# One encoder block on one core: the dense expert stage loads its weights two tiles at a time

## The chip, the core and the metric

The kernel runs on one core of a Trainium2 chip. The metric is the device time of one execution in microseconds (us), and a smaller one is better. The core's engines, with the profile's short names, are TensorE (PE, with its weight loads as PEld), VectorE (DVE), ScalarE (ACT), GpSimd (POOL) and SyncE (SP). SP does nothing here but issue DMAs, one after the other in a fixed order; POOL and ACT issue some too. All DMAs share 16 DMA engines.

## The reference, cut to what matters

The block normalizes x (512 frames of 2048 values), projects it, runs a recurrent mixer and a sparse attention, adds the result, and ends with an expert layer in which every frame uses 8 heads x 16 experts out of 16,384. The change lies in that last layer:

```python
def blk(args):                       # hx: frames, e: chosen experts, gt: their gates
    hx, e, gt = args
    act = jax.nn.gelu(jnp.einsum('nd,nhkd->nhk', hx, expert_u[e]), approximate=False)
    return jnp.einsum('nhk,nhkd->nd', gt * act, expert_v[e])
```

`expert_u` and `expert_v` are 16,384 x 2048 float32 each, 128 MB each.

## The kernel before

The kernel works in stages, one after the other: projections and mixers (to about 1695 us), routing (which experts each frame uses, to about 2250 us), then the dense stage to the end. The expert layer is split by frames. The first 176 frames (`NG`) are **gathered**: for each slot POOL fetches 128 expert rows of 8192 B, one row to a partition, into a tile `rows` by an indirect DMA (L1038), and DVE reduces them (L1048 for `expert_u`, L1060 for `expert_v`). The other 336 frames (`ND`) are **dense**: they are multiplied with all experts, and a gate matrix `G` with zeros for the experts that were not chosen selects.

The dense stage, `experts` (from L1240), goes through 16 groups of 8 tiles of 128 experts. Of a group, 6 expert tiles are computed here (2 of each 8 were done early, during routing, and their result comes back as `gel<-d_a`): `act` and `pieces` take 16 blocks of 128x128 weights of `pu` against the 336 frames into `mm` (L220 to L222), ACT applies Gelu, DVE multiplies with `G` (L1255), and the product is split into `Wh` and `Wl` (L233, L234). Then 16 output blocks `db` follow, each one weight tile of `pv` against the 8 `Wh`/`Wl` pairs into `wk` (L1290 to L1292), added to `accT` on DVE (L1297).

Both halves take their weights from `load_w`: SP loads a tile `raw` of 128 x 1024 float32, 512 KB, 4096 B to a partition (L201); ACT rounds it to `whi` (L204); DVE makes the rest `wlo` (L205). Each weight tile then feeds 24 matmuls: `whi` times the high part of the frames, `whi` times the low part, `wlo` times the high part, eight times. The high and low parts of the frames in the dense stage are `ph` and `pl`, packed copies of the routing stage's `h2h` and `h2l` (L1007 and L1008, four copies each).

Buffers come from pools. `wd`, opened at the head of `peer`, has 3 `raw`, 2 `whi` and 2 `wlo`; the query projections of routing (`wpq`) use it first, the dense stage goes on with it. When `h2` (which holds `h2h` and `h2l`) has been closed, a pool `wx` with 2 more `raw` and one more pair is opened in its place, so that the dense stage has 5 `raw` and 3 pairs; `load_w` counts tiles to say which pool serves which. The early expert tiles use a third pool `we`.

What sets the order: a scheduler orders each engine's instructions when the program is built, by when it thinks them ready; `high_priority(offset=100)` lets a weight tile's load and split go 100 instructions ahead. On the chip each engine then works strictly in that order and waits on semaphores. The gathered work is fed into the dense stage by `step`, which issues so many slots per weight tile (`rate`), each not before the last `wlo` (`issue_after(self.last)`). The gathers have 3 buffers `rows`.

Of the kernel before, what the change touches and what calls it, by code (L numbers as in the profile page):

```python
# [19 lines left out]
F32 = mybir.dt.float32  # L20
F32R = mybir.dt.float32r
# [3 lines left out]
AF = mybir.ActivationFunctionType  # L25
# [87 lines left out]
def layout(x, norm_mix_g, w_in, shift_mix, w0, w_decay_up, a0, w_icl_up, w_gate_up, k_k, k_a, r_k, ln_x_w, ln_x_b,  # L113
           kv_norm_g, w_uk, w_uv, rel_bias, w_branch_rwkv, w_branch_dsa, w_out, norm_ffn_g, w_peer_query,
           peer_sub_keys, peer_u, peer_v, norm_final_g):
    A = lambda a: np.ascontiguousarray(np.asarray(a))
    x, w_in = np.asarray(x)[0], np.asarray(w_in)[0]
    cols = columns()
    w = w_in[:, np.maximum(cols.reshape(-1), 0)].reshape(D, NTILE, 128)
    w[:, cols < 0] = 0  # L120
    vec = np.zeros((128, NVEC), np.float32)

    def put(n, a):
        o, k = VEC[n]
        vec[:, o:o + k] = np.asarray(a).reshape(k, 128).T
    put("gmix", norm_mix_g)
    sm = np.asarray(shift_mix)[0]
    c27 = cols[:27].copy()
    c27[(c27 >= 3360) | (c27 < 0)] = 0
    put("sm", sm[c27])  # L130
    for n, a in (("a0", a0), ("kk", k_k), ("ka", k_a), ("rk", r_k), ("lnw", ln_x_w), ("lnb", ln_x_b),
                 ("kvg", kv_norm_g), ("gffn", norm_ffn_g)):
        put(n, a)
    bt = np.asarray(rel_bias)[rel_bucket_table()]
    toep = bt[np.arange(512)[None, :] - np.arange(128)[:, None] - 384 + 511]
    kmajor = lambda m: A(m.reshape(-1, 128, m.shape[1] // 128, 128).transpose(2, 1, 0, 3))
    wbr = np.concatenate([np.asarray(w_branch_rwkv)[0], np.asarray(w_branch_dsa)[0]], 0)
    rank = lambda m: A(np.asarray(m)[0].transpose(1, 0, 2).reshape(2, 128, 1024).transpose(1, 0, 2))
    u = np.asarray(peer_u)[0].reshape(128, 128, 16, 128)
    v = np.asarray(peer_v)[0].reshape(128, 16, 8, 16, 128)  # L140
    return {
        "x": A(x), "xT": A(x.T.reshape(16, 128, T).transpose(1, 0, 2)),
        "w_in": A(w.reshape(16, 128, NTILE, 128).transpose(2, 1, 0, 3)),
        "vec": vec, "con": constants(),
        "w0": A(np.asarray(w0).reshape(1, 1024)), "gfin": A(np.asarray(norm_final_g).reshape(1, D)),
        "gffn": A(np.asarray(norm_ffn_g).reshape(1, D)),
        "wdec": A(np.asarray(w_decay_up)[0]), "wicl": A(np.asarray(w_icl_up)[0]), "wgate": A(np.asarray(w_gate_up)[0]),
        "wuk": rank(w_uk), "wuv": rank(w_uv), "toep": A(toep.transpose(2, 0, 1)),
        "wbr": kmajor(wbr),
        "wout": A(np.asarray(w_out)[0].reshape(8, 2, 128, 4, 512).transpose(3, 0, 2, 1, 4)),  # L150
        "wpq": kmajor(np.asarray(w_peer_query)[0]),
        "subk": A(np.asarray(peer_sub_keys)[0].reshape(16, 128, 128).transpose(2, 0, 1)),
        "pu": A(u.transpose(1, 3, 2, 0)),
        "pv": A(v.transpose(1, 3, 0, 2, 4)),
        "ru": A(np.asarray(peer_u)[0]), "rv": A(np.asarray(peer_v)[0]),
    }

# [10 lines left out]
class Kernel:  # L168
    def __init__(self, tc, io, out, dbg=None):
        self.tc, self.nc, self.io, self.out, self.dbg = tc, tc.nc, io, out, dbg or {}  # L170
        self.fins = ExitStack()
        self.wx, self.nw = None, 0
        self.blocks = ((0, 128), (1, 128), (2, ND - 256))

    def pool(self, name, bufs=1, **kw):
# [14 lines left out]
    def load_w(self, src, wp=None):  # L190

        nc = self.nc
        wp = wp or self.wp
        pr = ps = wp
        if self.wx and wp is self.wp:

            pr, ps = wp if self.nw % 5 < 3 else self.wx, wp if self.nw % 3 < 2 else self.wx
            self.nw += 1
        with self.tc.high_priority(offset=100):
            raw = pr.tile([128, 1024], F32, tag="raw", name="raw", bufs=3 if pr is wp else 2)  # L200
            nc.sync.dma_start(raw, src.rearrange("p a b -> p (a b)"))  # L201
            hi = ps.tile([128, 1024], F32R, tag="whi", name="whi")
            lo = ps.tile([128, 1024], F32R, tag="wlo", name="wlo")
            nc.scalar.activation(hi, raw, AF.Copy)  # L204
            self.last = nc.vector.tensor_tensor(lo, raw, hi.bitcast(F32), op=ALU.subtract).ins  # L205
        return hi, lo

    def gemm(self, *a, **k):
# [2 lines left out]
    def pieces(self, ps, w, xs, nk=16, wp=None):  # L211

        nc = self.nc
        for b in range(0, nk, 8):
            hi, lo = self.load_w(w[:, b:b + 8, :], wp)
            for j in range(8):
                k = b + j
                xh, xl = xs(k)
                s = slice(128 * j, 128 * j + 128)
                nc.tensor.matmul(ps, hi[:, s], xh, start=k == 0, stop=False)  # L220
                nc.tensor.matmul(ps, hi[:, s], xl, start=False, stop=False)  # L221
                nc.tensor.matmul(ps, lo[:, s], xh, start=False, stop=k == nk - 1)  # L222
                if j % 4 == 3:
                    yield
# [729 lines left out]
    def peer(self):  # L954
# [2 lines left out]
        v, sc = nc.vector, nc.scalar  # L957
        with ExitStack() as es:
            E = es.enter_context
            self.wp = E(self.pool("wd", 2))  # L960
            gk = self.gk = E(self.pool("gk"))
            self.eid, self.act_, self.gate = [[gk.tile([128, 128 // g[2]], dt, name=f"{n}{i}") for i, g in enumerate(GROUPS)]
                                              for n, dt in (("eid", I32), ("act", F32), ("gate", F32))]
            self.fold = gk.tile([128, 256], F32, name="fold")
# [41 lines left out]
            for a, b in ((0, 2), (2, 6), (6, 11), (11, 16)):  # L1006
                sc.activation(ph[:, a:b], hh[:, a:b, NG:T], AF.Copy)  # L1007
                v.tensor_copy(pl[:, a:b], hl[:, a:b, NG:T])  # L1008
            self.left.close()
            self.hs = lambda k: (ph[:, k], pl[:, k])  # L1010
            self.wx = E(self.pool("wx", 1))
            self.dp = E(self.pool("dense"))
            self.accT = self.dp.tile([128, 16, ND], F32, name="accT")
            self.experts()
# [224 lines left out]
    def experts(self):  # L1239
# [7 lines left out]
        for cg in range(16):  # L1247
            first, last = cg == 0, cg == 15
            G = dp.tile([128, ng, 8, 16], F32, name="G")
            nc.gpsimd.dma_start(G.rearrange("p g e t -> p g (e t)"), self.d_g[:, cg].rearrange("g p f -> p g f"))  # L1250
            W, wait = {}, []

            def gated(j, a):
                a3 = a.rearrange("p (g t) -> p g t", g=ng)
                v.tensor_tensor(a3, a3, G[:, :, j], op=ALU.mult)  # L1255
                wh = dp.tile([128, ND], F32R, name="Wh", bufs=8)
                wl = dp.tile([128, ND], F32R, name="Wl", bufs=8)
                self.split(a, wh, wl)
                W[j] = wh, wl

            js = list(range(8))
            if first:
                js = js[2:6] + js[0:2] + js[6:8]
            for j in js:
                e = 8 * cg + j
                if e in EARLY:
                    a = self.gel.tile([128, ND], F32, tag="gel", name="gel")
                    nc.scalar.dma_start(a, self.d_a[EARLY.index(e)])
                else:
                    a = run(self.act(e, self.mm()))  # L1270
                wait.append((j, a))
                while len(wait) > (2 if first and j in js[:6] else 0):
                    gated(*wait.pop(0))
                if e not in EARLY:
                    self.step(2)
            while wait:
                gated(*wait.pop(0))
            turn = iter(())
            if last:
                for _ in self.items:  # L1280
                    pass
                self.packed.close()
                turn = self.turned()
            for db in range(16):
                ps = self.wk()[:, 0:ND]
                hi, lo = self.load_w(io["pv"][cg, db])
                for j in js:
                    wh, wl = W[j]
                    s = slice(128 * j, 128 * j + 128)
                    mmul(ps, hi[:, s], wh, start=j == js[0], stop=False)  # L1290
                    mmul(ps, hi[:, s], wl, start=False, stop=False)  # L1291
                    mmul(ps, lo[:, s], wh, start=False, stop=j == js[-1])  # L1292
                a = self.accT[:, db]
                if first:
                    sc.activation(a, ps, AF.Copy)
                else:
                    v.tensor_tensor(a, ps, a, op=ALU.add)  # L1297
                next(turn, None)
                self.step()
# [63 lines left out]
```

## Time and profile before

| | before |
|---|---|
| median of 3 runs | 3996.01 us (3995.74 to 4000.47) |
| the profiled execution's own time | 3985.83 us |
| its span (first to last instruction) | 3984.1 us |
| PE busy | 3857.8 us, 97% of the span |
| DVE busy | 2843.3 us, 71% |
| ACT busy | 1398.7 us, 35% |
| DMA | 949.32 MB, mean 238 GB/s |

All numbers of the trace are from the one profiled execution, and its clock starts at the first instruction. A busy share over the whole span says little, since the stages have different limits. The dense stage lasts from 2250.70 us (its first matmul) to the end. `A <- B` in a table of waits reads: A sat idle until B was done.

### The profile page before, as it was taken

What the parts mean: (1) busy time and instruction counts of PE and PEld (TensorE: products, weight loads), DVE (VectorE), ACT (ScalarE), POOL (GpSimd) and SP (SyncE); (2) the same over time, 40 slices, a digit from 0 to 9 for tenths busy, and PEclk for the clock granted to TensorE, in tenths of its full rate; (3) what the DMA queues carried; (4) which work ended last, traced back from release to release, by engine and by line L of the source; (5) the groups of instructions that cost most, each with busy time, mean ns of one, the idle gap of its engine ahead of it and who ended that gap; (6) DMA issues with size and microseconds to landing.
All of it is one profiled execution on the core that took longest, in us unless ns stands there. A gap on an engine that the chain in (4) does not pass through costs nothing.

```text
span 3984.1 us, 57536 instructions
## 1 busy us (share of the span) xinstructions
PE 3857.8 (97%) x22241; PEld 3492.8 (88%) x22241; DVE 2843.3 (71%) x4742; ACT 1398.7 (35%) x2044; POOL 996.7 (25%) x965
## 2 busy tenths in 40 slices
PE   7999999999999999989999999999999999999998
PEld 6877778888887788878899999999999999999997
DVE  5445589444444643289987688989879889899985
ACT  4222323222224522242377533333333333333333
POOL 2000311010103400020166333333333334333320
PEclk9999999999999999999999999999999999999999
DMA  4343952233226443274377799999989999999994
GB/s 151 119 136 117 206 176 88 89 106 103 88 73 208 144 140 144 73 273 152 129 224 248 269 364 378 378 378 383 382 318 397 372 349 387 368 376 374 378 342 153
DMA packets 260275, 949.32 MB, mean 238 GB/s; under 512 B 28240, under 2 KB 79568, under 8 KB 211088
## 3 DMA queue, kind: packets, MB, share of 16 engines
q0 software_dynamic: 81840, 475.10, 32.0%
q1 hardware_dynamic: 130144, 442.62, 31.7%
q10 hardware_dynamic: 48016, 27.92, 2.4%
q8 instruction: 175, 2.87, 0.3%
q14 instruction: 100, 0.82, 0.1%
HBM read 867.56 MB, written 77.89 MB: 237 GB/s over the span
## 4 chain that ended last, share of the span: by engine, by line
PE 57%; issue 17%; DMA 10%; POOL 7%; DVE 7%; ACT 2%; SPq 0%; POOLq 0%; DVEq 0%; ACTq 0%
PE mm L221 10%; PE mm L222 10%; PE mm L220 10%; POOL rows L1038 6%; DMA rows<-in_rv_dram,eid 5%; PE wk L1292 3%; PE wk L1291 3%; PE wk L1290 3%; PE po L220 2%; PE po L221 2%; PE po L222 2%; DVE wlo L205 2%; PE wk L1220 2%; PE wk L876 2%; PE wk L878 1%
## 5 line engine op out<-in xcount | busy, mean ns | idle before, releaser
L204 ACT ACTIVATE whi<-raw 128x1024 fp32r<-128x1024 f32 x758 | 802.8, 1061 | 1820.4 <-PE mm L221 940.3
L205 DVE TENSOR_TENSOR wlo<-raw,whi 128x1024 fp32r<-128x1024 f32 x758 | 927.2, 1224 | 597.5 <-ACT whi L204 525.7
L1292 PE MATMUL wk<-Wh,wlo 128*128 128x336 f32 x2048 | 652.1, 319 | 13.3 <-DVE wlo L205 13.3
L1290 PE MATMUL wk<-Wh,whi 128*128 128x336 f32 x2048 | 651.6, 319 | 10.8 <-ACT Wh L233 10.8
L1291 PE MATMUL wk<-Wl,whi 128*128 128x336 f32 x2048 | 649.3, 317 | 4.2 <-DVE Wl L234 4.2
L222 PE MATMUL mm<-ph,wlo 128*128 128x336 f32 x1536 | 486.5, 317 | 1.8 <-DVE wlo L205 1.7
L220 PE MATMUL mm<-ph,whi 128*128 128x336 f32 x1536 | 484.9, 316 | 1.2 <-ACT ph L1007 1.2
L221 PE MATMUL mm<-pl,whi 128*128 128x336 f32 x1536 | 485.6, 316 | 0.0
L220 PE MATMUL mm<-xh,whi 128*128 128x512 f32 x1168 | 472.9, 405 | 1.6 <-ACT xh L353 1.5
L222 PE MATMUL mm<-xh,wlo 128*128 128x512 f32 x1168 | 468.3, 401 | 6.0 <-DVE wlo L205 6.0
L221 PE MATMUL mm<-xl,whi 128*128 128x512 f32 x1168 | 470.3, 403 | 0.6 <-POOL xl L355 0.5
L1060 DVE SCALAR_TENSOR_TENSOR out<-rows,act,out 128x2048 f32<-128x2048 f32 x173 | 405.7, 2345 | 46.9 <-DMA rows<-in_rv_dram,eid 46.1
L1038 POOL DMA_INDIRECT rows<-in_ru_dram,eid x176 | 272.2, 1547 | 664.7 <-DVE act L1048 484.3
L1048 DVE CUSTOM_DVE_ANT_0 rows<-rows,h2t 128x2048 f32<-128x2048 f32 x176 | 401.3, 2285 | 46.5 <-DMA rows<-in_ru_dram,eid 46.0
L1038 POOL DMA_INDIRECT rows<-in_rv_dram,eid x176 | 286.0, 1625 | 524.4 <-DVE out L1060 444.0
L1292 PEld LDWEIGHTS wk<-Wh,wlo 128*128 128x128 f32 x2048 | 387.1, 189 | 18.3 <-DVE wlo L205 17.1
L1290 PEld LDWEIGHTS wk<-Wh,whi 128*128 128x128 f32 x2048 | 386.2, 189 | 14.9 <-ACT Wh L233 14.2
L1291 PEld LDWEIGHTS wk<-Wl,whi 128*128 128x128 f32 x2048 | 386.9, 189 | 6.5 <-DVE Wl L234 5.6
L222 PEld LDWEIGHTS mm<-ph,wlo 128*128 128x128 f32 x1536 | 288.3, 188 | 2.7 <-DVE wlo L205 2.6
L220 PEld LDWEIGHTS mm<-ph,whi 128*128 128x128 f32 x1536 | 288.7, 188 | 1.8 <-ACT ph L1007 1.8
L221 PEld LDWEIGHTS mm<-pl,whi 128*128 128x128 f32 x1536 | 289.1, 188 | 0.0
L222 PEld LDWEIGHTS mm<-xh,wlo 128*128 128x128 f32 x1168 | 221.7, 190 | 60.2 <-DVE wlo L205 6.9
(441 smaller groups left out, 6348.1 us busy)
## 6 DMA issues: line engine op xcount, KB each, us to landing
raw<-in_pu_dram SPq DMA_DIRECT2D x256, 512.0 KB, 7.7
raw<-in_pv_dram SPq DMA_DIRECT2D x256, 512.0 KB, 8.0
raw<-in_w_in_dram SPq DMA_DIRECT2D x146, 512.0 KB, 3.8
d_g<-Gs ACTq DMA_DIRECT2D x21, 1024.0 KB, 6.8
G<-d_g POOLq DMA_DIRECT2D x16, 1344.0 KB, 15.1
raw<-in_wbr_dram SPq DMA_DIRECT2D x32, 512.0 KB, 4.0
raw<-in_wout_dram SPq DMA_DIRECT2D x32, 512.0 KB, 3.5
raw<-in_wpq_dram SPq DMA_DIRECT2D x32, 512.0 KB, 4.4
```

Of the source, the lines that this page charges most:

```text
L204: nc.scalar.activation(hi, raw, AF.Copy)
L205: self.last = nc.vector.tensor_tensor(lo, raw, hi.bitcast(F32), op=ALU.subtract).ins
L220: nc.tensor.matmul(ps, hi[:, s], xh, start=k == 0, stop=False)
L221: nc.tensor.matmul(ps, hi[:, s], xl, start=False, stop=False)
L222: nc.tensor.matmul(ps, lo[:, s], xh, start=False, stop=k == nk - 1)
L876: mmul(ps[tb], yh[:, k, t], hi[:, s], start=k == 0, stop=False)
L1038: nc.gpsimd.indirect_dma_start(out=r, out_offset=None, in_=table, in_offset=bass.IndirectOffsetOnAxis(ap=eid[:, s:s + 1], axis=0))
L1048: v.tensor_tensor_reduce(r, r, h, 1.0, 0.0, op0=ALU.mult, op1=ALU.add, accum_out=self.act_[i][:, s:s + 1])
L1060: v.scalar_tensor_tensor(o, r, act[:, s:s + 1], o, op0=ALU.mult, op1=ALU.add)
L1290: mmul(ps, hi[:, s], wh, start=j == js[0], stop=False)
L1291: mmul(ps, hi[:, s], wl, start=False, stop=False)
L1292: mmul(ps, lo[:, s], wh, start=False, stop=j == js[-1])
```

## The change

1. The dense stage gets a pool of its own, `wd2` (bufs 3), opened where `wx` was; `wx` and the counting are gone. `wd` is now opened after `gk` and closed after `h2`, so that `wd2` lies where `wd` and a part of `h2` were.
2. A load of the dense stage brings two weight tiles: `load_w2` loads `raw2`, 128 x 2048 float32, 1 MB, 8192 B to a partition, into one of 3 buffers, and splits its halves one after the other into `whi` and `wlo` (3 of each). For `pu` these are the two halves of one expert tile, which already lay together in memory; `pv` is laid out anew on the host so that two blocks `db` lie together.
3. The early tiles and the projections go on with 512 KB loads.

```diff
-        self.wx, self.nw = None, 0
+        self.double = False
...
-        pr = ps = wp
-        if self.wx and wp is self.wp:
-
-            pr, ps = wp if self.nw % 5 < 3 else self.wx, wp if self.nw % 3 < 2 else self.wx
-            self.nw += 1
         with self.tc.high_priority(offset=100):
-            raw = pr.tile([128, 1024], F32, tag="raw", name="raw", bufs=3 if pr is wp else 2)
+            raw = wp.tile([128, 1024], F32, tag="raw", name="raw", bufs=3)
             nc.sync.dma_start(raw, src.rearrange("p a b -> p (a b)"))
...
+            return self.parts_w(raw, wp)
+
+    def load_w2(self, src):
+
+        with self.tc.high_priority(offset=100):
+            raw = self.wp.tile([128, 2048], F32, tag="raw", name="raw2", bufs=3)
+            self.nc.sync.dma_start(raw, src)
+        for b in range(2):
+            with self.tc.high_priority(offset=100):
+                p = self.parts_w(raw[:, 1024 * b:1024 * b + 1024], self.wp)
+            yield p
...
-            self.wp = E(self.pool("wd", 2))
             gk = self.gk = E(self.pool("gk"))
+            wd = ExitStack()
+            self.wp = wd.enter_context(self.pool("wd", 2))
...
             self.left.close()
+            wd.close()
             self.hs = lambda k: (ph[:, k], pl[:, k])
-            self.wx = E(self.pool("wx", 1))
+            self.wp, self.double = E(self.pool("wd2", 3)), True
...
-                hi, lo = self.load_w(io["pv"][cg, db])
+                if db % 2 == 0:
+                    both = self.load_w2(io["pv"][cg, db // 2])
+                hi, lo = next(both)
```

Three places show what the change moves. The first is SP's queue during routing, where the query weights (`wpq`) end; `d_a` are the stores of early tiles. Before:

```order
156 L201 DMA raw<-in_wpq_dram 128x1024 x3
157 L201 DMA raw<-in_pu_dram 128x1024 x2
158 L1237 DMA d_a<-gel 128x336
159 L201 DMA raw<-in_pu_dram 128x1024 x6
160 L1237 DMA d_a<-gel 128x336
161 L201 DMA raw<-in_pu_dram 128x1024 x2
```

The same place after the change:

```order
156 L196 DMA raw<-in_wpq_dram 128x1024 x3
157 L196 DMA raw<-in_pu_dram 128x1024
158 L1249 DMA d_a<-gel 128x336
159 L196 DMA raw<-in_pu_dram 128x1024 x2
160 L1249 DMA d_a<-gel 128x336
161 L196 DMA raw<-in_pu_dram 128x1024 x2
```

Five loads fewer stand here: the first five that the dense stage puts into `wd`.

The second place is SP's queue where the dense stage begins, with the semaphores that each instruction waits for (an engine's name stands for its progress, `DMAHW` for a DMA's landing). Before:

```order
501 L201 DMA raw<-in_pu_dram 128x1024 [waits DMAHW4_49,DVE_49]
502 L1237 DMA d_a<-gel 128x336 [waits DMAHW3_49,Activation_49]
503 L1237 DMA d_a<-gel 128x336 [waits DMAHW5_49,Activation_49]
504 L1237 DMA d_a<-gel 128x336 [waits DMAHW6_49,Activation_49]
505 L201 DMA raw<-in_pu_dram 128x1024 [waits DVE_49,DMAHW7_49,PE_49,Activation_49]
506 L201 DMA raw<-in_pu_dram 128x1024 [waits DMAHW0_49]
507 L201 DMA raw<-in_pu_dram 128x1024 [waits DMAHW1_49,DVE_49]
```

After:

```order
497 L1249 DMA d_a<-gel 128x336 [waits DMAHW6_49,Activation_49]
498 L1249 DMA d_a<-gel 128x336 [waits DMAHW0_49,Activation_49]
499 L1249 DMA d_a<-gel 128x336 [waits DMAHW1_49,Activation_49]
500 L203 DMA raw_19064<-in_pu_dram 128x2048 [waits DVE_49,DMAHW2_49,PE_49,Activation_49]
501 L203 DMA raw_19128<-in_pu_dram 128x2048 [waits DMAHW3_49]
502 L203 DMA raw_19195<-in_pu_dram 128x2048 [waits DMAHW4_49]
503 L203 DMA raw_19264<-in_pu_dram 128x2048 [waits DMAHW5_49,DMAHW2_49,DVE_49]
```

In both, the row that waits for ACT, DVE and PE together (505 before, 500 after) waits in the built program for the last copies of `ph` and `pl` and for the last early matmul; before it is the sixth load of the dense stage, after it is the first.

The third place is ACT's order there. Before:

```order
999 L1231 ACTIVATE gel<-po 128x336 x2
1000 L1007 ACTIVATE ph<-h2h 128x672
1001 L1007 ACTIVATE ph<-h2h 128x1344
1002 L1007 ACTIVATE ph<-h2h 128x1680 x2
1003 L204 ACTIVATE whi<-raw 128x1024 x2
1004 L1231 ACTIVATE gel<-mm 128x336
```

After:

```order
998 L1243 ACTIVATE gel<-po 128x336 x2
999 L1018 ACTIVATE ph<-h2h 128x672
1000 L1018 ACTIVATE ph<-h2h 128x1344
1001 L1018 ACTIVATE ph<-h2h 128x1680 x2
1002 L213 ACTIVATE whi<-raw_19064 128x1024 x2
1003 L213 ACTIVATE whi<-raw_19128 128x1024 x2
```

Before, the first two splits of the dense stage stand further up, amid routing, and the third and fourth follow the copies; after, the first split follows the copies. From the second group of experts on, the orders of PE and DVE are the same before and after.

## Rows read from the trace of the kernel before

**Rows 1.** The page's part 2: busy tenths, 40 slices of the span.

```profile
PE   7999999999999999989999999999999999999998
DMA  4343952233226443274377799999989999999994
```

**Rows 2.** Windows, busy us (instructions) of PE, PEld, DVE, ACT, POOL; PEclk; DMA; GB/s.

```profile
2400.00:2800.00 400.00, 395.22 (x2559) 393.41 (x2558) 361.08 (x397) 133.51 (x159) 131.12 (x88) 1.00 0.98 378
```

**Rows 3.** Waits of PE, 2252 us to the end: total, times, longest.

```profile
PE wk L1292 <- DVE wlo L205: 13.3, 12, 3.0
PE wk L1290 <- ACT Wh L233: 10.8, 11, 2.1
PE wk L1291 <- DVE Wl L234: 4.2, 5, 1.4
PE mm L222 <- DVE wlo L205: 1.7, 2, 1.0
```

**Rows 4.** Waits of ACT, 2260 us to the end.

```profile
ACT whi L204 <- PE wk L1291: 613.8, 240, 7.4
ACT whi L204 <- PE mm L221: 296.9, 153, 2.7
...
ACT whi L204 <- DMA raw<-in_pu_dram: 4.4, 1, 4.4
```

**Rows 5.** Waits of DVE, 2260 us to the end.

```profile
DVE out L1060 <- DMA rows<-in_rv_dram,eid: 46.1, 22, 5.6
DVE rows L1048 <- DMA rows<-in_ru_dram,eid: 41.0, 24, 6.3
```

**Rows 6.** Waits of SP's queue, 2250 us to the end.

```profile
SPq L201 <- DVE wlo L205: 1472.8, 437, 10.8
```

**Rows 7.** Timeline where the dense stage begins: start, length, engine, operation.

```profile
2249.20 0.31 PE L222 MATMUL po<-h2h,wlo 128*128 128x336 f32 x1
...
2249.90 4.96 ACT L1007 ACTIVATE ph<-h2h 128x672 fp32r<-128x672 f32 x4
...
2250.70 0.42 PE L220 MATMUL mm<-ph,whi 128*128 128x336 f32 x1 [1.19 <-ACT ph L1007]
...
2251.12 0.32 PE L222 MATMUL mm<-ph,wlo 128*128 128x336 f32 x1
...
2254.88 8.14 SPq L201 DMA_DIRECT2D raw<-in_pu_dram  x4
2254.89 1.06 ACT L204 ACTIVATE whi<-raw 128x1024 fp32r<-128x1024 f32 x1
...
2255.99 1.23 DVE L205 TENSOR_TENSOR wlo<-raw,whi 128x1024 fp32r<-128x1024 f32 x1 [1.48 <-ACT whi L204]
...
2260.35 1.06 ACT L204 ACTIVATE whi<-raw 128x1024 fp32r<-128x1024 f32 x1 [4.40 <-DMA raw<-in_pu_dram]
```

**Rows 8.** Line L201 from 2253 to 2256 us: the loads issued there and their landing.

```profile
L201 SPq DMA_DIRECT2D raw<-in_pu_dram x2: 333/378/424, 2254.9 to 2255.3; - x2
...
DMA to landing us min/median/max: 5.4/5.8/6.3
```

**Rows 9.** Windows around PE's fall to 0.50 of its clock at 2305.6 us.

```profile
2305.60:2309.00 3.40, 3.40 (x14) 3.40 (x13) 0.92 (x3) 0.86 (x1) 2.07 (x2) 0.50 1.03 398
2309.00:2314.60 5.60, 5.60 (x38) 5.60 (x38) 5.37 (x5) 3.23 (x6) 0.90 (x2) 1.00 1.02 333
```

**Rows 10.** DMA from 2250 us: queues (packets, MB, share of 16 engines), issues (us to landing).

```profile
q0 software_dynamic: 54096, 374.10, 55.5%
q1 hardware_dynamic: 64464, 236.26, 36.3%
...
raw<-in_pv_dram SPq DMA_DIRECT2D x256, 512.0 KB, 8.0
...
rows<-in_rv_dram,eid POOLq DMA_INDIRECT x176, 9.6
rows<-in_ru_dram,eid POOLq DMA_INDIRECT x152, 9.6
```

More of the change, by code (lines that the diff above doesn't have):

```diff
@@ L139, in layout @@
     u = np.asarray(peer_u)[0].reshape(128, 128, 16, 128)
-    v = np.asarray(peer_v)[0].reshape(128, 16, 8, 16, 128)
+    v = np.asarray(peer_v)[0].reshape(128, 16, 8, 8, 2, 128)
     return {
@@ L153, in layout @@
         "pu": A(u.transpose(1, 3, 2, 0)),
-        "pv": A(v.transpose(1, 3, 0, 2, 4)),
+        "pv": A(v.transpose(1, 3, 0, 4, 2, 5).reshape(16, 8, 128, 2048)),
         "ru": A(np.asarray(peer_u)[0]), "rv": A(np.asarray(peer_v)[0]),
@@ L193, in load_w, with parts_w @@
         wp = wp or self.wp
-        pr = ps = wp
-        if self.wx and wp is self.wp:
-            pr, ps = wp if self.nw % 5 < 3 else self.wx, wp if self.nw % 3 < 2 else self.wx
-            self.nw += 1
         with self.tc.high_priority(offset=100):
-            raw = pr.tile([128, 1024], F32, tag="raw", name="raw", bufs=3 if pr is wp else 2)
+            raw = wp.tile([128, 1024], F32, tag="raw", name="raw", bufs=3)
             nc.sync.dma_start(raw, src.rearrange("p a b -> p (a b)"))
[L202 to L205, printed above, removed]
+            return self.parts_w(raw, wp)
[7 more added lines that the diff above has]
+            yield p
+    def parts_w(self, raw, wp):
+        nc = self.nc
+        hi = wp.tile([128, 1024], F32R, tag="whi", name="whi")
+        lo = wp.tile([128, 1024], F32R, tag="wlo", name="wlo")
+        nc.scalar.activation(hi, raw, AF.Copy)
+        self.last = nc.vector.tensor_tensor(lo, raw, hi.bitcast(F32), op=ALU.subtract).ins
         return hi, lo
@@ L213, in pieces @@
         nc = self.nc
+        both = self.load_w2(w.rearrange("p a b -> p (a b)")) if self.double else None
         for b in range(0, nk, 8):
-            hi, lo = self.load_w(w[:, b:b + 8, :], wp)
+            hi, lo = next(both) if both else self.load_w(w[:, b:b + 8, :], wp)
             for j in range(8):
```

## The prediction

> **What bounds the kernel now.** I first read the busy slices, to see what kind of limit the changed stage has. In the dense stage, from slice 23 on, PE stands at nine tenths or more and so do the DMA engines [rows 1]; 400 us of it show PE busy 395 us, DVE 361 us and the DMA engines 98% at 378 GB/s [rows 2]. Three resources are nearly full, so what ends PE's waits has to be read, not the shares. PE waits 30.0 us in all after the stage has begun (13.3 + 10.8 + 4.2 + 1.7): 15.0 us for `wlo`, 15.0 us for `Wh` and `Wl` [rows 3]. The rest of the stage is matmuls, which the change leaves alone.
>
> Are those 15.0 us for `wlo` late weight loads? ACT's waits say no. Ahead of `whi` ACT waits some 910 us for PE to give a pair back (613.8 + 296.9), and for a weight load once, 4.4 us, at the start [rows 4]. SP, which issues the loads, stands 1472.8 us waiting for a free `raw`, 437 times [rows 6]. So weights are there in time. What makes `wlo` late is DVE's order: DVE sits before late gathered rows 46.1 + 41.0 = 87.1 us in 46 places [rows 5], and a `wlo` that stands behind such a reduction comes late with it. The gathers are the transfers that matter in this stage; the weight loads matter through what they take from the gathers.
>
> **The change, part by part.**
>
> The number of issues: 448 loads of 512 KB become 224 of 1 MB. SP's issue time is no price, since SP waits [rows 6]; this counts nothing. Nor do the splits change: the same ACT and DVE instructions on the same 128x1024, and still three pairs. The depth is about the same too: 5 buffers of 512 KB before, 3 of 1 MB now, and a buffer comes free after its second half is split, so the next load of that buffer is wanted five tiles later, as before.
>
> The beginning of the stage is where the change costs. Today five loads stand amid routing in SP's order, into `wd`, which is free once the query weights are done; two of those tiles are split long before the stage begins. So PE starts on the dense stage 1.19 us after it could, as soon as the first quarter of `ph` is copied, at 2250.70 us, and runs on the two ready tiles while the copies, the next loads and splits proceed [rows 7]. A tile is 24 matmuls, and 2250.70 to 2251.12 is two steps, about 0.15 us apart after the first; two tiles are about 7.4 us, and with the third, split from 2254.89 us on, about 11 us. The load issued at 2254.88 us feeds the `whi` of 2260.35 us [rows 7], just as this cover ends.
>
> After the change the first load of the stage waits for the last copy, as row 500 of SP's order shows. The copies end at 2249.90 + 4.96 = 2254.86 us, and the load that waits for them today is issued at 2254.88 us [rows 7]. Nothing early in the stage is left to cover it. When does 1 MB land? The two loads of 512 KB issued at 2254.9 and 2255.3 us land 5.4 and 6.3 us later [rows 8], together 1 MB by about 2261.6 us; I take that for the first 1 MB (bounds: 5.4 us as for the first half, 2260.3 us, and 9.6 us, the median of a gather [rows 10], the same 1 MB in the full stage, 2264.5 us). Then `whi` takes 1.06 us and `wlo` 1.23 us [rows 7]: with 0.04 us between them and the same ahead, `whi` is ready at 2262.7 us and `wlo` at 2263.9 us. The first two matmuls need only `whi`; the third needs `wlo` and started at 2251.12 us today. The loss is 2263.9 - 2251.1 = **12.8 us**, between 11.5 and 15.7 by the bounds. The following tiles do not add: their splits run while PE works, and the second and third megabyte are queued at once (rows 501 and 502 wait only for a DMA long done).
>
> TensorE's clock comes on top. PE would idle from 2249.5 us [rows 7] for about 13 us. At 2305.6 us today the granted clock stands at 0.50, the lower level, for 3.4 us: 14 matmuls in 3.40 us, then 38 in 5.60 us at the full level, so 23 would have fitted and 9 x 0.147 us = 1.3 us are lost [rows 9]. I count one such step, **1.3 us** (bounds: none, and three).
>
> What leaves routing: five loads, two `whi` and two `wlo`, beside early matmuls that fill PE. I count nothing; the most it can give back is the two `whi`, 2 x 1.06 = 2.1 us [rows 7].
>
> The rest of the stage, 1,650 us: DMA is shared differently, and the trace holds bounds for both signs. Bytes are the same. The weights' queue (q1) takes 36.3% of 16 engines for 236.26 MB, the gathers' (q0) 55.5% for 374.10 MB [rows 10]: in 1734 us that is 42.6 and 41.2 engine-us for each MB. If weights in 8192 B pieces move as cheaply as the gathered rows of 8192 B, 235 MB x 1.4 / 16 = 21 us of DMA time are saved, 1.2 points of 97%. That helps late rows a little. Against it, a gather that meets a weight load now meets twice as much: 1 MB moves in about 1.05 x 42.6 / 16 = 2.8 us, 512 KB in 1.4 us, so one that meets a load wholly is delayed 1.4 us more, though it meets half as many. With rows as late as they are now in 46 of 328 places (22 + 24 of 176 + 152) [rows 5, 10], spreading hurts more than it helps. The floor is that all 30.0 us of waits vanish; for the top see the second rival. I take **0**, since the order of PE and DVE there is the same and the weight loads are off the chain.
>
> The Trainium skill, page "DMA: Bandwidth & Descriptors", section "Queues, rings and completion order", says that each DMA engine takes turns between the queues, a packet at a time. By it, weights of 8192 B against rows of 8192 B would take one half of an engine where 4096 B took a third, so the gathers would slow down: the second rival rather than zero. The same page, section "Bandwidth", advises batches of 1 MiB and more; by it the first rival would win. The trace cannot tell them apart, as no weight load of 1 MB is in it.
>
> The sum: 12.8 + 1.3 - 0 + 0 = 14.1 us. On the profiled execution, 3985.83 us, that is 3999.9 us. The median of the runs is 10.2 us above that execution, and I add to the median: 3996.0 + 14.1 = **4010 us**.
>
> **Rivals.**
>
> First, the other side: fewer late rows. The DMA time saved lets the gathers land sooner, DVE no longer stands before them, and PE's waits go. If all go: 14.1 - 30.0 = -15.9 us, 3980 us. For it: DMA is at 97%, where a point matters. Against it: half of PE's waits are for `Wh` and `Wl`, at the turn from `pu` to `pv`, where three instructions of DVE and ACT follow each other; rows are not their only cause. It turns the sign only from 14.1 us on, nearly half of all waits; faster by 0.2% (8 us) needs 22 of 30.
>
> Second, starved gathers. If late rows double, from 46 to 92 at the same 1.9 us each (87.1 / 46) [rows 5], DVE waits 87 us more; PE today waits 30.0 us for 87.1 us of these, a third, so 30 us more: 3996 + 14 + 30 = 4040 us. For it: 98% of the DMA engines busy and 9.6 us from issue to landing with three buffers [rows 2, 10]. Against it: total bytes fixed, weights wanted at PE's pace alone, and DVE idle a tenth of the time [rows 2].
>
> Third, the beginning costs nothing: the loss of cover is made good, because waits saved later or the 2.1 us in routing take it back, or because the first megabyte lands and is split sooner than I count. Then within 8 us of 3996. For it: 6 us of saved waits are enough. Against it: the order leaves PE no other work there.
>
> **How the numbers follow.** A measurement of this kernel can tell about 0.2%, 8 us, from no change. My forecast, 4004 to 4022 us, gets 0.60; starved gathers (4022 us and more, about 4040) 0.17; a beginning that is made good (within 8 us) 0.16; fewer late rows beyond that 0.07. So faster 0.07, same 0.16, slower 0.77. The range runs from 3998 us, where the third rival keeps half of its chance, to 4036 us, within the second, and leaves out about 0.2.
>
> **What would show it.** Right: one gap of PE of 12 to 15 us at about 2250 us, ended by `whi` or `wlo`, with the first `raw2` issued right after the last copy and landing 5 to 9 us later; PE's later waits between 15 and 45 us; DVE's waits for rows near 87 us; the clock at 0.50 for some us after the gap. Wrong: no such gap, or one under 5 us (third rival); DVE's waits for rows under 40 us with PE's later waits under 10 us (first); rows landing over 11 us after issue and DVE waiting 150 us or more for them (second). ACT waiting for `raw2` in the middle of the stage would say that three buffers of 1 MB are too shallow, which I have counted at nothing.

## The result and the profile after

| | before | after |
|---|---|---|
| median | 3995.88 us, 4 runs | 4029.40 us, 4 runs (4026.96 to 4031.71) |
| the profiled execution's own time | 3985.83 us | 4031.28 us |
| its span | 3984.1 us | 4029.5 us |

The change makes the kernel slower: ratio 1.0089, 95% interval 1.0075 to 1.0104, some 33.5 us of the medians. Beside the kernel before on a second chip, where that one has a median of 3991.37 us, the ratio was 1.0102 (1.0082 to 1.0122). The forecast of 14 us had the sign and a part of the size. Later comparisons are given as ratios to runs of the kernel before on the same chip.

Where does the time go? First PE's waits, from 2240 us to the end (total, times, longest):

```profile
PE wk L1304 <- ACT Wh L243: 26.9, 13, 3.6
PE wk L1306 <- DVE wlo L214: 16.3, 15, 2.3
PE mm L230 <- ACT whi L213: 11.6, 1, 11.6
PE wk L1305 <- DVE Wl L244: 5.0, 3, 2.3
PE mm L232 <- DVE wlo L214: 4.0, 5, 1.6
```

The third line is new and has one single wait: the start of the dense stage. The other four are those of [rows 3]; 0.3 us of the last also belongs to the start. Without the start they come to 51.9 us, against 30.0 us. So PE loses time by waiting in two ways: about 12 us once, and about 22 us spread over the stage, most of it (16.1 us) before the first matmuls that need a new `Wh`.

A third loss is not a wait. PE is busy for 3869.5 us instead of 3857.8 us with the same number of matmuls, 11.7 us more: between 2253 and 3950 us its granted clock stands at 0.50, the lower level, for 44 us in all, against 10 us before. Waits and busy time together make up the 45.4 us between the two traced spans. The medians differ by 12 us less, since the traced execution of the kernel before was 10 us faster than its median; the parts of the trace are therefore not parts of the 33.5 us one by one.

Then DVE's waits for gathered rows, from 2260 us:

```profile
DVE rows L1060 <- DMA rows<-in_ru_dram,eid: 55.3, 34, 7.4
DVE out L1072 <- DMA rows<-in_rv_dram,eid: 50.0, 38, 6.2
```

105.3 us in 72 places, against 87.1 us in 46 [rows 5]. The rows have become late more often, though no more of them are fetched over the whole kernel (queue q0 moves 81,840 packets in both).

The weights come in time as before. Among ACT's waits, in the same stretch, the weight loads stay small, and SP still waits for a free buffer:

```profile
ACT whi L213 <- DMA raw<-in_pu_dram: 6.6, 2, 5.2
```

```profile
SPq L203 <- DVE wlo L214: 1593.4, 218, 14.3
```

The two DMA queues from 2250 to 4030 us (packets, MB, share of 16 engines):

```profile
q0 software_dynamic: 54240, 375.15, 55.6%
q1 hardware_dynamic: 32928, 238.87, 34.9%
```

The weights' queue has half as many packets as in [rows 10], and a MB in it takes 0.349 x 16 x 1780 / 238.87 = 41.6 engine-us (microseconds of one of the 16 DMA engines) instead of 42.6. The larger pieces are a little cheaper, and the kernel is slower all the same.

### The start

The timeline where the dense stage begins, as in [rows 7]:

```profile
2255.74 1.28 SPq L203 DMA_DIRECT2D raw<-in_pu_dram  x3
2256.25 1.49 POOL L1262 DMA_DIRECT2D G<-d_g  x1 [23.80 <-ACT ph L1018]
2260.91 2.00 ACT L213 ACTIVATE whi<-raw 128x1024 fp32r<-128x1024 f32 x2 [5.20 <-DMA raw<-in_pu_dram]
2262.00 2.36 DVE L214 TENSOR_TENSOR wlo<-raw,whi 128x1024 fp32r<-128x1024 f32 x2 [6.63 <-ACT whi L213]
...
2262.02 0.65 PE L230 MATMUL mm<-ph,whi 128*128 128x336 f32 x1 [11.64 <-ACT whi L213]
...
2263.28 0.65 PE L232 MATMUL mm<-ph,wlo 128*128 128x336 f32 x1 [0.33 <-DVE wlo L214]
```

SP issues its first three loads of 1 MB once the copies have ended; the first is in use 5.2 us later; `whi` and `wlo` follow, and PE sat idle 11.64 + 0.33 us in front of its first three matmuls.

### One turn from `pu` to `pv`

The larger loss is best seen at one place, the turn in group 13. The kernel before:

```profile
3584.54 2.35 DVE L1060 SCALAR_TENSOR_TENSOR out<-rows,act,out 128x2048 f32<-128x2048 f32 x1 [1.10 <-DMA rows<-in_rv_dram,eid]
...
3586.81 1.22 DVE L205 TENSOR_TENSOR wlo<-raw,whi 128x1024 fp32r<-128x1024 f32 x1
...
3587.94 0.50 DVE L1255 TENSOR_TENSOR gel<-gel,G 128x336 f32<-128x336 f32 x1
3588.48 0.48 ACT L233 ACTIVATE Wh<-gel 128x336 fp32r<-128x336 f32 x1 [3.43 <-DVE gel L1255]
...
3589.01 0.58 PE L1290 MATMUL wk<-Wh,whi 128*128 128x336 f32 x2 [1.56 <-ACT Wh L233]
```

The same instructions after the change:

```profile
3626.80 2.35 DVE L1072 SCALAR_TENSOR_TENSOR out<-rows,act,out 128x2048 f32<-128x2048 f32 x1 [2.40 <-DMA rows<-in_rv_dram,eid]
3629.07 1.22 DVE L214 TENSOR_TENSOR wlo<-raw,whi 128x1024 fp32r<-128x1024 f32 x1
...
3630.20 0.50 DVE L1267 TENSOR_TENSOR gel<-gel,G 128x336 f32<-128x336 f32 x1
3630.74 0.48 ACT L243 ACTIVATE Wh<-gel 128x336 fp32r<-128x336 f32 x1 [5.21 <-DVE gel L1267]
...
3631.27 0.58 PE L1304 MATMUL wk<-Wh,whi 128*128 128x336 f32 x2 [3.32 <-ACT Wh L243]
```

Order and durations are the same. The gathered row is 2.40 us late instead of 1.10, and everything behind it on DVE, on ACT and on PE moves with it: ACT waits 1.78 us longer, and PE 1.76 us, 3.32 instead of 1.56. This row gives 1.30 us of that; by the rest, about 0.5 us, DVE was already further behind ACT when it came to the row. A part is paid twice, as the windows right behind it show (columns as in [rows 2]):

```profile
3632.00:3635.40 3.40, 3.40 (x15) 3.40 (x14) 1.54 (x2) 0.11 (x1) 2.43 (x2) 0.50 1.10 378
3635.40:3640.00 4.60, 4.60 (x31) 4.60 (x30) 4.12 (x5) 2.02 (x2) 0.00 (x0) 1.00 0.86 248
```

After the wait PE is granted the lower clock (0.50): 15 matmuls in 3.40 us, where 23 fit at the pace of the next line.

### The profile page after: what moved, and what is told of

It reads as the page before. It is cut to its first block, busy times and chain, and to the rows that moved or that the text cites. A ratio compares the mean times of both kernels' runs of the same rounds, so it can differ in the third digit from the quotient of the medians.

```text
span 4029.5 us, 56934 instructions
## 1 busy us (share of the span) xinstructions
PE 3869.5 (96%) x22241; PEld 3502.8 (87%) x22241; DVE 2846.0 (71%) x4742; ACT 1396.9 (35%) x2044; POOL 994.0 (25%) x965
## 3 DMA queue, kind: packets, MB, share of 16 engines
q0 software_dynamic: 81840, 475.10, 32.3%
## 4 chain that ended last, share of the span: by engine, by line
PE 44%; issue 17%; DMA 8%; POOL 7%; DVE 4%; ACT 2%; SPq 0%; POOLq 0%; DVEq 0%; ACTq 0%
PE mm L231 6%; PE mm L232 6%; PE mm L230 6%; POOL rows L1050 6%; DMA rows<-in_rv_dram,eid 5%; PE wk L1304 3%; PE wk L1306 3%; PE wk L1305 3%; PE po L230 2%; PE po L231 2%; PE po L232 2%; PE wk L1232 2%; PE wk L886 1%; PE wk L888 1%; PE wk L887 1%
```

## The experiments

The theory to test: (A) the start costs what the trace shows, and the rest comes from the 8192 B pieces (a piece is what a load writes into one partition in one run), which make gathered rows late. Its rivals: (B) the rest follows from the late start or the new pool, and (A2) it follows from 1 MB being freed and filled at once, whatever the pieces.

### e1: the pool alone, with 512 KB loads

```diff
...
-            raw = wp.tile([128, 1024], F32, tag="raw", name="raw", bufs=3)
+            raw = wp.tile([128, 1024], F32, tag="raw", name="raw", bufs=6 if self.double and wp is self.wp else 3)
...
-                if db % 2 == 0:
-                    both = self.load_w2(io["pv"][cg, db // 2])
-                hi, lo = next(both)
+                hi, lo = self.load_w(io["pv"][cg, db])
```

> The change's pool alone: wd2 where the change has it, but six raw of 512 KB, one tile to a load, 4096 B to a partition, and pv laid out as before. The start of the dense stage is the changed kernel's (its first load waits for the last copy of ph), the weights' pieces are those of before. Theory A (the start costs what it showed, some 13 us, and the rest of the loss comes from 1 MB loads of 8192 B pieces that make gathered rows late): about 4008 us, PE's waits after 2270 us 25 to 35 us, DVE's waits for rows about 87 us. Theory B (the rest comes from the new pool or from the late start itself): about 4029 us, PE's later waits about 50 us.

Measured: 4004.56 us, ratio 1.0035 (1.0022 to 1.0048). PE's waits from 2240 us:

```profile
PE wk L1301 <- ACT Wh L242: 15.6, 11, 3.1
PE wk L1303 <- DVE wlo L214: 13.0, 12, 4.4
PE mm L229 <- ACT whi L213: 10.7, 1, 10.7
PE wk L1302 <- DVE Wl L243: 3.5, 3, 1.4
PE mm L231 <- DVE wlo L214: 3.4, 4, 1.7
```

The start is there (10.7 us; the first load is only 512 KB), the later waits are 35 us, and rows cost DVE 95 us in 55 places. The pool and the late start explain 0.35% of 0.9 to 1.0%, and B falls as the whole of the rest.

### e2: 1 MB buffers, filled by two DMAs of 4096 B a partition

```diff
-            self.nc.sync.dma_start(raw, src)
+            for b in range(2):
+                self.nc.sync.dma_start(raw[:, 1024 * b:1024 * b + 1024], src[:, 1024 * b:1024 * b + 1024])
```

> The changed kernel, but each raw2 of 1 MB is filled by two DMAs of 512 KB, each 4096 B to a partition. Buffers, pairs, orders of PE and DVE as in the change. Theory A1 (pieces of 8192 B take a larger share of each DMA engine from the gathers): late rows fall back to those of before, DVE's waits for rows about 87 us, about 4010 us. Theory A2 (it is the freeing and filling of two tiles at once, a burst of 1 MB, whatever the pieces): stays at about 4029 us, DVE's waits for rows about 105 us or more.

Measured: 4006.87 us, ratio 1.0039 (1.0026 to 1.0052), like e1. DVE's waits for rows, from 2270 us:

```profile
DVE out L1073 <- DMA rows<-in_rv_dram,eid: 43.4, 28, 5.6
DVE rows L1061 <- DMA rows<-in_ru_dram,eid: 38.3, 25, 5.6
```

81.7 us in 53 places, less than before the change. Buffers, pairs and PE's order are those of the change, and 1 MB still comes free and is asked for at once, so A2 falls. What differs is the piece, and with it the size of a single DMA, 512 KB instead of 1 MB; this run does not part the two.

### e4 and e9: the start of before, with either piece

In e4 `wd` stays open and gives the dense stage its first four tiles by 512 KB loads, of which some stand amid routing as before; from the fifth tile on, 1 MB loads go into `raw2` of a later pool.

```diff
...
-            raw = self.wp.tile([128, 2048], F32, tag="raw", name="raw2", bufs=3)
+            raw = self.wx.tile([128, 2048], F32, tag="raw", name="raw2", bufs=3)
...
-        both = self.load_w2(w.rearrange("p a b -> p (a b)")) if self.double else None
+        both = self.load_w2(w.rearrange("p a b -> p (a b)")) if self.double and self.nw >= 4 else None
...
```

> 1 MB loads with the start of before: wd stays open with its 3 raw of 512 KB and 2 pairs and gives the dense stage its first four tiles by 512 KB loads, of which five or so stand amid routing; from the fifth tile on 1 MB loads into three raw2 of a pool opened after h2 was closed. Theory A (start 13 us, the rest from 1 MB loads): no gap of PE at 2250 us, later waits about 50 us as in the change, about 4015 us. Theory B (the rest follows from the late start): about 3996 us with later waits about 30 us.

Measured: 4020.06 us, ratio 1.0080 (1.0066 to 1.0095). The gap at the start is gone (1.2 us), and the later waits are those of the change:

```profile
PE wk L1308 <- ACT Wh L249: 28.1, 13, 3.2
PE wk L1310 <- DVE wlo L220: 13.9, 16, 2.3
PE mm L238 <- DVE wlo L220: 5.0, 4, 2.7
PE wk L1309 <- DVE Wl L250: 4.9, 4, 1.7
```

DVE's waits for rows, from 2270 us, are the longest but for those of e3, 115.2 us in 69 places:

```profile
DVE rows L1064 <- DMA rows<-in_ru_dram,eid: 58.6, 31, 6.9
DVE out L1076 <- DMA rows<-in_rv_dram,eid: 56.6, 38, 7.1
```

The loss was larger than the 19 us that theory A had left for it, some 32 us. Was it the piece, or e4's buffers? e9 is e4 with the two DMAs of e2 for each 1 MB.

> e4 (the start covered, 1 MB buffers) with each 1 MB filled by two DMAs of 512 KB, 4096 B to a partition; PE's order that of e4. Theory A1 (pieces of 8192 B take the gathers' share): back to the kernel before, 0.999 to 1.002 of it, DVE's waits for rows about 87 us instead of 115, PE's later waits about 30 us instead of 52. Rival (e4's loss of 0.8% comes from its buffers or its order): stays at 1.008.

Measured: 3995.89 us, ratio 1.0012 (1.0002 to 1.0021). Rows cost DVE 82.8 us and PE's later waits are 32.8 us. Between e4 and e9, with one start, one set of buffers and one order of PE, one load of 1 MB in pieces of 8192 B costs 0.7% more than two of 512 KB in pieces of 4096 B.

These two traces also show in what way rows are late. The median time from issue to landing hardly differs: 9.8 and 9.5 us for the two tables in e4, 9.7 and 9.5 us in e9. But of the 328 gathers from 2260 us on, 83 take more than 11 us in e4, and 53 in e9, as many as in the kernel before. The gathers are not slower as a whole; their times spread, and more of them are late.

### e7: the change itself on the second chip

> The changed kernel itself once more, on the same chip as the others, to stand beside e4 (its 1 MB loads without the lost start: 1.0080) and e1 and e2 (its start with 4096 B pieces: 1.0035 and 1.0039). If the two losses add up: 1.0115 to 1.012, some 46 us. If they do not: 1.009 as at first, some 34 us.

Measured: 4031.50 us, ratio 1.0102 (1.0082 to 1.0122). Its trace repeats the first one: DVE waits 101.5 us for rows in 65 places, and PE's later waits are 47 us. The two losses taken singly, 0.35% (e1) and 0.80% (e4), make 1.15%; that lies inside this interval, and above that of the first comparison, 1.0075 to 1.0104. Whether they overlap by a few microseconds stays open.

### e8: smaller pieces

If a larger piece takes from the gathers, a smaller one should give to them. e8 is the kernel before with two DMAs of 2048 B a partition for each 512 KB of the dense stage; the orders of PE, DVE and POOL stay.

```diff
-            nc.sync.dma_start(raw, src.rearrange("p a b -> p (a b)"))
+            src = src.rearrange("p a b -> p (a b)")
+            if self.wx and wp is self.wp:
+                for b in range(2):
+                    nc.sync.dma_start(raw[:, 512 * b:512 * b + 512], src[:, 512 * b:512 * b + 512])
+            else:
+                nc.sync.dma_start(raw, src)
```

> The kernel before, each 512 KB load of the dense stage issued as two DMAs of 512 columns, so 2048 B to a partition; orders of PE, DVE, ACT and POOL unchanged. Theory A1 (a queue's share of a DMA engine goes with the size of its pieces): the gathers get more, rows come earlier than before, DVE's waits for rows 50 to 70 us instead of 87, PE's later waits 15 to 25 us, 5 to 12 us faster; unless pieces of 2048 B cost so much more DMA time (over 50 engine-us for each MB) that rows come later. Rival (pieces do not matter under 4096 B): no change.

Measured: 3976.53 us, ratio 0.9960 (0.9949 to 0.9972), though a MB of weights now takes more DMA time, 0.369 x 16 x 1780 / 236.29 = 44.5 engine-us. DVE's waits for rows:

```profile
DVE rows L1053 <- DMA rows<-in_ru_dram,eid: 31.2, 18, 4.5
DVE out L1065 <- DMA rows<-in_rv_dram,eid: 29.0, 16, 4.2
```

So the kernel moves against DMA efficiency and with the size of the piece, on both sides of 4096 B. The weights pay for it: ACT, which waited for them once before [rows 4], now waits some 110 us for loads in 35 places, of which PE feels 1.4 us.

```profile
ACT whi L209 <- DMA raw<-in_pv_dram: 91.8, 29, 5.6
```

| piece of a weight load | kernel | DVE's waits for rows, places | PE's later waits | ratio |
|---|---|---|---|---|
| 2048 B | e8 | 60.2 us, 34 | 22.4 us | 0.9960 |
| 4096 B | before | 87.1 us, 46 | 30.0 us | 1 |
| 4096 B | e9 | 82.8 us, 53 | 32.8 us | 1.0012 |
| 8192 B | e4 | 115.2 us, 69 | 51.9 us | 1.0080 |

With the runs that have the late start, 4096 B has 82 to 95 us of DVE's waits and 30 to 35 us of PE's (before, e1, e2, e9), and 8192 B has 101 to 115 us and 47 to 52 us (the change, e7, e4). In each of these runs a DMA is 128 pieces, so its size goes with the piece.

### e5 and e6: a fourth buffer for rows

The other end of the chain: if late rows are the cause, a deeper queue of rows should hide them. In the dense stage every fourth row goes into one more buffer, in memory that is free there.

```diff
...
+            self.rows2 = E(self.pool("rows2", 1))
...
+            p = self.rows2 if self.rows2 and n[0] % 4 == 3 else self.rows
...
```

The orders of DVE, PE and POOL shift in a few places with it. e5 is the kernel before with it:

> The kernel before with a fourth buffer for gathered rows (8192 B to a partition, in the dense stage alone, on the free memory behind its pool). If late gathered rows are what makes DVE late and PE wait: DVE's waits for rows fall from 87 us to under 40, PE's later waits from 30 us to 20 or less, the time falls by some 10 us. If PE's waits come from the order of DVE and ACT alone: no change of the time within 0.2%.

Measured: 3955.94 us, ratio 0.9910 (0.9893 to 0.9928). DVE's waits for rows fall to 30.0 us in 14 places:

```profile
DVE rows L1055 <- DMA rows<-in_ru_dram,eid: 16.0, 6, 3.8
DVE out L1067 <- DMA rows<-in_rv_dram,eid: 14.0, 8, 2.3
```

PE's waits from 2240 us, those of the stage:

```profile
PE wk L1297 <- ACT Wh L234: 3.9, 3, 2.1
PE wk L1299 <- DVE wlo L206: 2.4, 3, 1.2
...
PE wk L1298 <- DVE Wl L235: 1.3, 1, 1.3
...
PE mm L223 <- DVE wlo L206: 0.2, 1, 0.2
```

e6 is the change with it:

> The changed kernel with the same fourth buffer for rows. Theory A (1 MB loads of 8192 B pieces cost by making rows late): the fourth buffer hides most of it, DVE's waits for rows under 60 us, PE's later waits 30 us or less instead of 52, the start still lost: 14 us above the kernel before. Rival (the loss of the later stage is not the rows'): stays at 33 us above it.

Measured: 3973.68 us, ratio 0.9954 (0.9938 to 0.9970). DVE waits 39.7 us for rows, PE's later waits are 9.8 us, near e5's 7.8 us, and the gap at the start remains (11.5 us). With four buffers the 8192 B piece costs PE about 2 us of waits instead of 22, and e6 lies 0.44% above e5, about what the start alone costs in e1.

e5's median falls by 35 us, more than the 22 us of waits that it saves. The two traces differ by 29.6 us (spans of 3984.1 and 3954.5 us): besides the waits, PE is busy for 7.1 us less (3857.8 and 3850.7 us). It is granted the full clock from 2300 to 3850 us, while in the kernel before the clock fell three times for 3.4 us, as in [rows 9]. The other 6 us lie between the traced execution of the kernel before and the median of its runs on this chip.

### e10: both helps at once

> Both helps together, on the kernel before: a fourth buffer for rows and weight loads in pieces of 2048 B. e5 left PE 8 us of later waits, so by theory A1 there is little more to have: 0.989 to 0.991 of the kernel before, later waits under 8 us, DVE's waits for rows under 25 us. If the smaller pieces cost DMA time that now matters: 0.992 or more.

Measured: 3978.25 us, ratio 0.9962 (0.9948 to 0.9976): worse than e5 by half a per cent, no better than e8. Waits for rows cost DVE only 5.1 us in 7 places; instead ACT, from 2270 us, waits for weights:

```profile
ACT whi L210 <- DMA raw<-in_pv_dram: 201.0, 67, 6.3
...
ACT whi L210 <- DMA raw<-in_pu_dram: 20.9, 6, 6.1
```

PE's later waits are 24 us, against 7.8 us in e5, with the orders of PE, DVE and POOL of e5. The weights are now the late ones. The expectation had named this side, smaller pieces that cost DMA time which now matters. The trace bears it out so far: a MB of weights takes 0.372 x 16 x 1780 / 236.29 = 44.8 engine-us against 41.6 in e5, and from 2300 to 3800 us the DMA engines are 99% busy against 97%. That the gathers, with a fourth row in flight, also take more from small pieces is possible; no run here parts the two. Either way, help for the rows can be overdone.

### e3: two DMAs of 64 partitions

```diff
-            self.nc.sync.dma_start(raw, src)
+            for b in range(2):
+                self.nc.sync.dma_start(raw[64 * b:64 * b + 64], src[64 * b:64 * b + 64])
```

> The changed kernel, but each raw2 of 1 MB is filled by two DMAs of 64 partitions, 512 KB each, still 8192 B to a partition. Theory A1 (8192 B pieces): stays at about 4029 us. Theory A2 (1 MB at once): also about 4029 us, since both halves are issued one behind the other. A third theory, that it is the size of the single DMA: about 4010 us.

Measured: 4693.41 us, ratio 1.1759 (1.1743 to 1.1774), which no theory expected. The run tells nothing of the size of a single DMA, since the form has a price of its own (last section). So whether the piece counts or the size of the whole DMA stays open: in e2, e8 and e9 both are halved together.

## Why the prediction was right or wrong

**What bounds the kernel: right.** The weights did not become the late ones, in spite of 1 MB loads and three buffers; rows did, and DVE's order carried it on. e5 shows how much hung on them.

**The start: right, and nearly well sized.** The first 1 MB was in use 5.2 us after its issue, where the forecast had 6.7 us. The third matmul started at 2263.28 us against 2251.12 us, 12.2 us later, of which 0.9 us had arisen before the copies. So the gap cost 11.3 us where 12.8 us was forecast, a little below the lower bound of 11.5 us. The clock made up for it: it stood at 0.50 until 2266.7 us, and matmuls started every 0.28 us instead of every 0.15 us, which cost about 2 us (an estimate from these two paces) instead of 1.3 us. e1 and e2, which have this start, show 1.0035 and 1.0039, 14 and 16 us, of which 3 to 5 us are more of the later waits.

**The pieces: the step that failed is "I take 0".** The prediction saw that a gather meets larger loads less often and that such spreading hurts, and priced it at nothing, because orders were unchanged and weights off the chain. The term is 32 us taken alone (e4), and 0.7% between e4 and e9. In the traces it shows as spread: 83 gathers of more than 11 us instead of 53, at nearly the same median.

By the rule of the Trainium skill ("DMA: Bandwidth & Descriptors", "Queues, rings and completion order"), DMA engines take turns between queues packet by packet; an estimate from it is that a piece twice as large doubles what a weight load takes in its turn, if a packet holds as many pieces as before. DVE's waits go that way over 2048, 4096 and 8192 B, with 60, 82 to 95 and 101 to 115 us; the median landing time of a gather does not, between 4096 and 8192 B. So the turns are not shown to be the mechanism: no run here shows the packets of one DMA engine in order. The advice of the Trainium skill on the same page ("Bandwidth"), to make DMAs 1 MiB or more, holds for the weights' own cost, 41.6 for 42.6 engine-us for each MB, and not for this kernel's time.

**The second rival: the right direction with the wrong sizes.** It had rows late in 92 places, DVE waiting 87 us more, and PE a third of that. Measured: 72 places, 18 us more of DVE's waits, and 22 us more of PE's. Its sign, DVE waiting 150 us or more, was not met. PE's waits do not follow DVE's by an average ratio: at the turn to `pv` in group 13, ACT and PE lost the whole 1.8 us by which DVE had come later. The time, 4029.4 us, lies above the forecast's own 4004 to 4022 us. That it lies inside the wider range is owed to the part that this rival covered, late rows, and not to the reasoning of the forecast; as far as that goes it was luck.

**The first rival: wrong in its cause.** Larger pieces save DMA time, as it said, but rows were late more often all the same. **The third:** routing gave nothing back; the copies began 0.9 us later than before.

**The clock: too small.** I counted one fall after the gap, 1.3 us, and at most three. After the gap the clock fell seven more times by 3950 us, close behind waits as at 3632 us above, and PE's busy time grew by 11.7 us.

## What to carry to other kernels

Where two DMA streams share busy DMA engines, the form of one stream's loads can make the other one late. Here that was the size of their pieces, together with the size of a DMA. Before making a load larger, ask which stream's lateness ends in a wait of the bounding engine, and keep the other one's pieces no larger than it needs. Look at the late transfers and not at the median: the median hardly moved here. If the late stream has few buffers, try one more first: the fourth row buffer gave 0.9% here, smaller pieces 0.4%, and both together less than the buffer alone. And a pool that is moved into memory which is freed late loses the loads that ran ahead of it: look in the order for what stands before the stage's first wait.

## What the runs showed of the hardware that was not expected

In e3, loads of 64 partitions were costly for both queues. The same bytes in the same 8192 B pieces, half of the partitions to a DMA, filled the DMA engines with less work. From 2400 to 2800 us (queue: packets, MB, share):

```profile
q0 software_dynamic: 9367, 65.74, 60.2%
q1 hardware_dynamic: 6029, 39.44, 39.8%
```

A MB of weights took 0.398 x 16 x 400 / 39.44 = 64.6 engine-us instead of 41.6, and a MB of gathered rows, whose form is unchanged, 58.6 instead of 42.2; the engines were full at 266 GB/s, against 368 GB/s in the same window after the change. Both queues slow down together, which suggests that what they wait for is shared. Which part that is was not tried.
